# Value products taken unit by unit, index scores in PSUM, and three smaller edits in a three-branch decoder layer

## Chip, cores and metric

One Trainium2 chip, one core. The metric is the device time of one execution in microseconds. A run of the kernel before takes 537.79 us (median of three: 534.98, 537.79, 538.72).

## What is computed

One decoder layer over 512 tokens of width 1024. One input projection feeds three mixers side by side, whose results are gated, projected, merged and normalised. Cut to what this change is about:

```python
u = x @ w_in + b_in                               # split by columns into the parts below
# A: pooling with trailing windows 2, 4, 8, 16 on four groups of 128 channels
pooled = mean_over_window(a_x) - a_x              # the first w-1 tokens divide by their position
y_a = (pooled @ pool_w + b) * scale * silu(a_z)
# B: an indexer picks 128 keys for each query
score = sum_h relu(iq_h @ ik.T) * iw_h            # 8 index heads
sel = top_k(causal(score))
y_b = softmax(bq @ bk[sel].T / 8) @ bv[sel] * silu(b_z)     # 8 heads of 64
# C: compressed blocks, selected blocks and a window, 2 groups of 4 heads
k_cmp, v_cmp = mlp(blocks of 32 tokens)           # 31 blocks per group
o = g0 * softmax(cq @ k_cmp.T) @ v_cmp + g1 * softmax(cq @ ks.T) @ vs + g2 * softmax(cq @ kw.T) @ vw
y_c = o * silu(c_z)
m = sum over branches of sigmoid(g_branch) * (y_branch @ w_proj_branch)
out = layernorm(ALPHA * x + m @ w_o)
```

## The kernel before

**Dense work.** The projection's weights come as 53 tiles of 128 x 1024 (`load_w`): a DMA into `w_st`, a high part `w_h` by ACT (L93), a low part `w_l` by GpSimd (L95; by DVE for the first twelve). Every fp32 product is three matmuls (`mm3`, L68 to L70): high by high, high by low, low by high. Such a group of three, 512 columns wide, is the smallest piece of dense work; the projections are `d`, those of the merge `pp`, those of the output `wo`.

**Attention units.** A unit is one group of four heads and one block `j` of 128 queries, for a branch of C (names `c`, two branches `br`) or for B (names `b`). `Unit.front` makes the scores in PSUM (L442, `qkc`/`qkb`), DVE masks them and takes the least (L444), ACT exponentiates with that as bias (L449), DVE computes `r`, one over the sum (L453 to L457), ACT and DVE split the probabilities into two f16 parts (L461, L463), and SP's queue transposes them with a DMA (L470) into `ptc` or `ptb`, of which there are two buffers. A unit with `j` of 2 or 3 is made in two subunits of two heads. `Unit.back` multiplies the transposed parts by the values (L480) into an accumulator `acc`. `finish` (L535, DVE) reads the accumulator and writes `yb` or `yc`. All accumulators are two halves, used in turn, of one PSUM tile `ACC` that fills one bank:

```python
    ACC = pv.tile([128, 2, 2, 128], F32, name="acc2")
    turn = [0]
```

`Compressed` rides on the first branch of C: its scores (L506, or L502 and L503 for the last block), one exp over 128 x 32 blocks of four heads (L512, L513), and products of its own (L530) into the same accumulator with `VC`, the compressed values with the heads on the diagonal (L397).

**Order.** PE's order is the order of the program (`manual_schedule`). The order on the other engines is worked out by a scheduler from it. Dense work and merging lie in a stream `F` as generators that yield after every group; between pieces of attention `F.step(n)` issues n of them. The work list runs c units of group 0 (`j` 3, 2, 1, 0, each with two branches), c of group 1, then b units of group 0 (`j` 0 to 3) and of group 1. `flush` issues the backs: always two units together, once the second of the two is `LAG` = 2 subunits old. For C the two are the branches of one accumulator; for B they are two accumulators, b0 with b1 and b2 with b3, and the finish of the first stands between their products:

```python
            for _, un, (kind, g, j, br) in pair:
                for _ in un.back(br == 0):
                    n += 1
                if kind == "b":
                    finish(un.acc, j, zb[g], YB[g])
```

**Other places.** `index_scores` (L283): per index head a product of 128 x n into one of four PSUM banks (L290), a relu by ACT into an SBUF tile `rel` (L292), and an accumulation by DVE (L294, L296). The DVE top-k rounds (L305, L306, L309) are spread between subunits. `compress_v` (L382) writes `VC` with six DVE multiplications by a mask. `pool_x` (L555) makes the pooled group; its first w − 1 columns are made apart and copied in by DVE (L574).

Of the kernel before, what the change touches and what calls it, by code (L numbers as in the profile page):

```python
# [7 lines left out]
F32 = mybir.dt.float32  # L8
# [3 lines left out]
AF = mybir.ActivationFunctionType  # L12
OP = mybir.AluOpType
# [12 lines left out]
I_IQ, I_KK, I_CQ, I_KC, I_VC, I_CZ, I_BQ, I_BZ, I_AX, I_AZ, I_G = (  # L26
    1, 3, 5, 9, 10, 11, 15, 19, 23, 27, 31)
NTILES = I_G + 24
SMALL = (("posk", 32), ("posv", 32), ("pool_b", 4), ("pool_scale", 4), ("bmask", 4), ("rcnt", 16), ("rowv", 1),
         ("mcmp", 128), ("ident", 128))  # L30
EARLY = (0, I_KK)

# [2 lines left out]
def trunk(ctx, tc, a, out, dbg=None):  # L35
    nc = tc.nc
# [11 lines left out]
    def big(tag, name, dt=F32, shape=(128, 2, 512)):  # L48
        return bp.tile(list(shape), dt, tag=tag, name=name, bufs=BUFS[tag])
# [7 lines left out]
    def qps(name):  # L57
        return pq.tile([128, 512], F32, tag="pq", name=name)
# [18 lines left out]
    small = {}  # L77
# [23 lines left out]
    ps = qps("idle")  # L101
# [25 lines left out]
    bias = const("bias")  # L127
# [157 lines left out]
    def index_scores(j):  # L285
        n = (j + 1) * 128
        acc = cp.tile([128, n], F32, name=f"acc{j}")
        for h in range(8):
            ps = qps(f"is{j}{h}")[:, :n]
            nc.tensor.matmul(ps, QI[h][:, (j - 1) * 128:j * 128], KI[:, :n], start=True, stop=True)  # L290
            rel = big("b", "rel", F32, (128, 512))[:, :n]
            nc.scalar.activation(rel, ps, AF.Relu)  # L292
            if h == 0:
                nc.vector.tensor_scalar(acc, rel, IW[:, j, 0:1], None, op0=OP.mult)  # L294
            else:
                nc.vector.scalar_tensor_tensor(acc, rel, IW[:, j, h:h + 1], acc, op0=OP.mult, op1=OP.add)  # L296
            yield
        dg = acc[:, j * 128:n]
        nc.vector.tensor_add(dg, dg, cmask[:, 384:512])
        dbg(f"score{j}", acc)  # L300
        negm[j] = acc
# [11 lines left out]
    KCH = cp.tile([128, 2, 32], F32R, name="kch")  # L313
    KCL = cp.tile([128, 2, 32], F32R, name="kcl")
    VC = [cp.tile([128, 2, 4, 64], BF, name=f"vc{p}") for p in range(3)]

    CP = {}

# [62 lines left out]

    def compress_v():  # L382
        HH, HL, w2h, w2l = CP["v"] + W2[1]
        bmask = small["bmask"]
        v32 = sp.tile([128, 2, 64], F32, name="vc32", bufs=1)
        ps = dps("vc")[:, :128].rearrange("p (g d) -> p g d", g=2)
        for g in range(2):
            mm3(ps[:, g], HH[:, g].rearrange("p r n -> p (r n)"), HL[:, g].rearrange("p r n -> p (r n)"),
                w2h, w2l, True, True)
        nc.vector.tensor_scalar(v32, ps, vscale, 0.5, op0=OP.mult, op1=OP.mult)  # L390
        for p in range(3):
            v1 = sp.tile([128, 2, 64], BF, name="vc1", bufs=2)
            nc.vector.tensor_copy(v1, v32)
            if p < 2:
                nc.vector.tensor_sub(v32, v32, v1)
            for g in range(2):
                nc.vector.tensor_mul(VC[p][:, g], v1[:, g, None, :].to_broadcast([128, 4, 64]),  # L397
                                     bmask[:, :, None].to_broadcast([128, 4, 64]))
        yield


# [83 lines left out]
    class Compressed:  # L485
# [5 lines left out]
        def begin(self, j, Q, K):  # L491
            self.j = j
            self.s = sp.tile([128, 4, 32], F32, name="cs", bufs=1)
            self.mx = sm("cmx", 4, 2)
            self.scale = 0.125 if j == NT - 1 else -1.0
            if j == NT - 1:
                ps = dps("sc")[:, :128].rearrange("p (h n) -> p h n", h=4)
                for h in range(4):
                    q = Q[h // 2][:, h % 2, j * 128:(j + 1) * 128]
                    for z in range(2):  # L500
                        nc.tensor.matmul(ps[:, h], q, K[:, z, :32], start=z == 0, stop=z == 1)
                nc.vector.tensor_add(self.s, ps, mcmp[:, j, None].to_broadcast([128, 4, 32]))  # L502
                nc.vector.tensor_reduce(self.mx[:, :4], self.s, AX.X, OP.max)  # L503

        def score(self, h, ps):
            nc.vector.tensor_tensor_reduce(self.s[:, h], ps, mcmp[:, self.j], -0.125, 3e38, OP.add, OP.min,  # L506
# [2 lines left out]
        def probs(self):  # L509
            g, j, s = self.g, self.j, self.s  # L510
            den, r = sm("cden", 4, 2), sm("cr", 4, 2)
            nc.vector.tensor_sub(s, s, self.mx[:, :4, None].to_broadcast([128, 4, 32]))  # L512
            nc.scalar.activation(s, s, AF.Exp, scale=self.scale)  # L513
            nc.vector.tensor_reduce(den, s, AX.X, OP.add)
            nc.vector.reciprocal(r, den)
            nc.vector.tensor_mul(r, r, GS[:, j, 12 * g:12 * g + 12:3])
            if j == 0:
                nc.vector.tensor_scalar(r, r, rowv, None, op0=OP.mult)
            nc.vector.tensor_mul(s, s, r[:, :, None].to_broadcast([128, 4, 32]))
            p = sp.tile([128, 2, 4, 32], F16, name="cp", bufs=1)  # L520
            nc.scalar.activation(p[:, 0], s, AF.Copy)
            nc.vector.tensor_sub(p[:, 1], s, p[:, 0])
            self.pt = sp.tile([128, 2, 128], F16, name="cpt", bufs=2)
            nc.sync.dma_start_transpose(self.pt, p.rearrange("p z h n -> p (z h n)"))
# [32 lines left out]
    def pool_x(g):  # L557
        w = 2 << g
        ps, b = yield from dense(I_AX + g)
        x0 = big("b", "x0", F32, (128, 512))  # L560
        with tc.high_priority():
            hi(x0, ps, b)
        cur = x0
        for i in range(g + 1):
            nxt = big("b", "xs", F32, (128, 512))
            sft = 1 << i
            nc.gpsimd.tensor_add(nxt[:, sft:], cur[:, sft:], cur[:, :S - sft])
            nc.gpsimd.tensor_copy(nxt[:, :sft], cur[:, :sft])
            cur = nxt
        e = sm("pe", 16, 1)  # L570
        nc.vector.tensor_mul(e[:, :w - 1], cur[:, :w - 1], PL["rcnt"][:, :w - 1])
        nc.vector.tensor_sub(e[:, :w - 1], e[:, :w - 1], x0[:, :w - 1])
        nc.vector.scalar_tensor_tensor(x0, cur, 1.0 / w, x0, op0=OP.mult, op1=OP.subtract)
        nc.vector.tensor_copy(x0[:, :w - 1], e[:, :w - 1])  # L574
        ph = PL["x", g] = big("t", "ph", F32R)
        split(ph[:, 0], ph[:, 1], x0)

# [160 lines left out]
    mcmp, rowv = small["mcmp"].rearrange("p (j n) -> p j n", j=NT), small["rowv"]  # L738
# [38 lines left out]
    backs = []  # L777
    accs, cmps = {}, {}
    nsub = 0

    def flush(limit):

        while backs and (limit == 1000 or len(backs) > 1 and backs[1][0] <= limit):
            pair, n = backs[:2], 0
            del backs[:2]
            if limit == 1000:
                F.step(12)
            for _, un, (kind, g, j, br) in pair:
                if kind == "c":
                    F.until(("vscales",), ("compress_v",), ("f_zc", g, 0), ("f_zc", g, 1))  # L790
                else:
                    F.until(("f_zb", g, 0), ("f_zb", g, 1))
            for _, un, (kind, g, j, br) in pair:
                for _ in un.back(br == 0):
                    n += 1
                if kind == "b":
                    finish(un.acc, j, zb[g], YB[g])
                elif br == 1:
                    cmps[g, j].back(un.acc)
                    finish(un.acc, j, zc[g], YC[g])  # L800
                    if j == 0:
                        flags.add(f"c{g}")
                        if g == 1:
                            split_y(2, YC)
            F.step(0.3 * n)

    for w in work:
        kind, g, j, br = w
        if kind == "c":
# [6 lines left out]
            if br == 0:  # L816
                cmps[g, j] = Compressed(g)
            un = Unit(f"c{g}{j}{br}", accs[w[:3]], j, qc[g], kk[g][br], cmask[:, (3 - j) * 128:],
                      1 + 2 * br + g, gv[:, 4 * g:4 * g + 4, 1 + br], None if br else cmps[g, j])
        else:  # L820
# [3 lines left out]
            if j:  # L824
                tk_until(j)
            un = Unit(f"b{g}{j}", psum_acc(), j, qb[g], KB[0], cmask[:, 384:] if j == 0 else negm[j],
                      0, None)
        for u in range(un.nsub):
# [4 lines left out]
            nsub += 1  # L833
            F.step(2)
            flush(nsub - LAG)
        backs.append((nsub, un, w))
    flush(1000)
    F.rest()
    POOL[0] = False
# [60 lines left out]
    for t in range(NT):  # L900
        last = t == NT - 1
        for c0, c1 in ((512, 768), (768, 1024)) if last else ((512, 1024),):
            ps = dps("wo")
# [5 lines left out]
        mv, ve, y, e = sm("mv", 2), sm("ve", 1), sm("rs", 1), sm("nw", 1)  # L909
# [8 lines left out]
        if not last:  # L918
            c = cs.pop()
# [11 lines left out]
def layout(v):  # L931
    import numpy as np
    v = {k: np.asarray(x) for k, x in v.items()}
    x, w, b = v["x"][0], v["w_in"][0], v["b_in"][0]
# [17 lines left out]
    c = np.ascontiguousarray  # L952
# [15 lines left out]
    for n in "kv":  # L968
        p = v["cmp_pos_" + n][0].T
# [4 lines left out]
    f4 = np.float32  # L974
    t = np.arange(128)
    r["cmask"] = np.concatenate([np.zeros((128, 384), f4), np.where(t[None] <= t[:, None], 0, NEG).astype(f4)], 1)
    r["ident"] = np.eye(128, dtype=f4)
    n = np.arange(32)
    tt = (np.arange(4)[None, :] * 128 + t[:, None])[:, :, None]
    r["mcmp"] = np.where((16 * n + 31 <= tt) & (n < 31), 0, NEG).astype(f4)  # L980
    r["rowv"] = (t >= 31).astype(f4)[:, None]
    r["bmask"] = (t[:, None] // 32 == np.arange(4)[None]).astype(f4)
    r["rcnt"] = c(np.broadcast_to((1.0 / np.arange(1, 17)).astype(f4), (128, 16)))
    r["small"] = np.concatenate([r.pop(k).reshape(128, n) for k, n in SMALL], 1)
    return {k: c(x) for k, x in r.items()}
# [16 lines left out]
```

## Time and profile before

| | us |
|---|---|
| median of three runs | 537.79 |
| profiled execution | 536.65 |
| its span | 534.9 |
| outside the span | 1.75 |
| mean granted TensorE clock, share of full speed | 0.982 |

The profile follows one execution. A row of busy time says how long an engine worked in the span; a row of a wait says which engine stood idle ahead of which instruction, and whose instruction ended that idle time. PE is TensorE's matmul, PEld its weight load beside it. In names, buffer numbers are left out.

### The profile page before, as it was taken

How to read it: one execution, taken by the hardware profiler on the slowest of the kernel's cores; microseconds unless marked ns; L12 is line 12 of the kernel's file. 1: busy time of each engine (PE TensorE's matmuls, PEld its weight loads, DVE VectorE, ACT ScalarE, POOL GpSimd, SP SyncE). 2: the span in 40 equal slices, each digit the busy share in tenths (PEclk: the TensorE clock that was granted, in tenths of full speed). 3: DMA queues.
4: the chain of work that ended last, by engine and by line, in shares of the span. 5: the costliest groups of instructions: out<-in, count | busy, mean ns of one | idle time of the engine just before them, and what ended most of it. 6: DMA issues, size and time to landing. Idle time of an engine off the chain costs nothing. (4 is left out here: it accounts for less than half of the span.)

```text
span 534.9 us, 7764 instructions
## 1 busy us (share of the span) xinstructions
PE 510.4 (95%) x2718; PEld 423.7 (79%) x2718; DVE 380.2 (71%) x928; ACT 278.4 (52%) x561; POOL 218.5 (41%) x190
## 2 busy tenths in 40 slices
PE   8999999999999998999998995999899999999993
PEld 5899878888888886788887884887787888887883
DVE  5774798898769898997898879565653345554276
ACT  6783465667655666565546564575553245342000
POOL 0425433436553756153534534227651212116043
PEclk9999989999999999999999998899999999999997
DMA  8622331363854434364545636256444435463012
GB/s 286 256 79 80 112 126 60 87 148 86 183 139 123 119 85 117 63 181 124 140 121 104 132 110 145 49 138 138 119 119 134 141 137 187 148 205 110 1 69 89
DMA packets 82135, 66.72 MB, mean 125 GB/s; under 512 B 67184, under 2 KB 68656, under 8 KB 82096
## 3 DMA queue, kind: packets, MB, share of 16 engines
q1 hardware_dynamic: 74912, 40.54, 28.5%
q0 software_dynamic: 7184, 25.69, 16.1%
q8 instruction: 21, 0.34, 0.3%
q14 instruction: 18, 0.15, 0.1%
HBM read 47.87 MB, written 2.10 MB: 93 GB/s over the span
## 5 line engine op out<-in xcount | busy, mean ns | idle before, releaser
L68 PE MATMUL d<-xh,w_h 128*128 128x512 f32 (+1 forms) x424 | 167.5, 395 | 2.6 <-ACT z L153 2.2
L69 PE MATMUL d<-xl,w_h 128*128 128x512 f32 (+1 forms) x424 | 165.8, 391 | 0.0
L70 PE MATMUL d<-xh,w_l 128*128 128x512 f32 (+1 forms) x424 | 165.5, 390 | 0.0
L95 POOL TENSOR_TENSOR w_l<-w_st,w_h 128x1024 fp32r<-128x1024 f32 x41 | 99.5, 2428 | 127.1 <-ACT w_h L93 120.4
L68 PEld LDWEIGHTS d<-xh,w_h 128*128 128x128 f32 x424 | 80.5, 190 | 18.3 <-ACT z L153 2.6
L70 PEld LDWEIGHTS d<-xh,w_l 128*128 128x128 f32 x424 | 80.3, 189 | 16.9
L69 PEld LDWEIGHTS d<-xl,w_h 128*128 128x128 f32 x424 | 80.4, 190 | 14.1
L93 ACT ACTIVATE w_h<-w_st 128x1024 fp32r<-128x1024 f32 x53 | 56.2, 1060 | 36.9 <-DMA w_st<-in_wt_dram 20.5
L449 ACT ACTIVATE qkc<-qkc,nb 128x512 f32<-128x512 f32 (+3 forms) x64 | 32.0, 501 | 49.8 <-DVE nb L444 32.0
L95 POOL TENSOR_TENSOR wp_l<-wp_st,wp_h 128x512 fp32r<-128x512 f32 x16 | 20.8, 1297 | 48.3 <-ACT wp_h L93 48.3
L641 POOL TENSOR_TENSOR m<-m,tg 128x512 f32<-128x512 f32 x12 | 17.5, 1457 | 54.2 <-DVE tg L615 54.0
L463 DVE SCALAR_TENSOR_TENSOR pc<-qkc,r,pc 128x512 f16<-128x512 f32 (+3 forms) x64 | 32.4, 544 | 8.2 <-ACT pc L461 7.9
L461 ACT ACTIVATE pc<-qkc,r 128x512 f16<-128x512 f32 (+3 forms) x64 | 29.5, 525 | 15.1 <-DVE r L457 7.2
L444 DVE CUSTOM_DVE_ANT_0 qkc<-qkc,cmask 128x512 f32<-128x512 f32 (+3 forms) x64 | 31.2, 493 | 2.9 <-PE qkc L442 2.5
L449 ACT ACTIVATE qkb<-qkb,nb 128x128 f32<-128x128 f32 (+3 forms) x32 | 16.0, 499 | 23.1 <-DVE nb L444 22.8
L92 POOL DMA_DIRECT2D w_st<-in_wt_dram x41 | 23.3, 569 | 9.9 <-POOL w_l L95 5.9
L70 PE MATMUL wo<-woh,ml 128*128 128x512 f32 (+1 forms) x72 | 26.4, 367 | 0.6 <-DVE ml L65 0.6
L69 PE MATMUL wo<-wol,mh 128*128 128x512 f32 (+1 forms) x72 | 26.3, 366 | 0.0
L68 PE MATMUL wo<-woh,mh 128*128 128x512 f32 (+1 forms) x72 | 26.3, 365 | 0.0
L306 DVE MATCH_REPLACE8 acc<-m,acc 128x256 f32<-128x256 f32 (+2 forms) x48 | 25.9, 541 | 0.0
L305 DVE MAX8 m<-acc 128x8 f32<-128x256 f32 (+2 forms) x48 | 25.2, 548 | 0.1
L68 PE MATMUL pp<-yh,wp_h 128*128 128x512 f32 x64 | 25.1, 392 | 0.0
(249 smaller groups left out, 1015.3 us busy)
## 6 DMA issues: line engine op xcount, KB each, us to landing
w_st<-in_wt_dram POOLq DMA_DIRECT2D x41, 512.0 KB, 3.7
w_st<-in_wt_dram SPq DMA_DIRECT2D x12, 512.0 KB, 4.4
wp_st<-in_wp_dram POOLq DMA_DIRECT2D x16, 256.0 KB, 3.0
wo_st<-in_wo_dram SPq DMA_DIRECT2D x8, 512.0 KB, 3.5
xst<-in_xT_dram SPq DMA_DIRECT2D x8, 256.0 KB, 4.8
wp_st<-in_wp_dram SPq DMA_DIRECT2D x8, 256.0 KB, 2.6
z<-in_x_dram SPq DMA_DIRECT2D x4, 512.0 KB, 5.1
wvst<-in_wve_dram SPq DMA_DIRECT2D x4, 320.0 KB, 7.1
```

Source lines behind the costliest of these rows:

```text
L68: nc.tensor.matmul(ps, wh, rh, start=start, stop=False)
L69: nc.tensor.matmul(ps, wh, rl, start=False, stop=False)
L70: nc.tensor.matmul(ps, wl, rh, start=False, stop=stop)
L92: (nc.gpsimd if POOL[0] else nc.sync).dma_start(st, src)
L93: nc.scalar.activation(h[:, :n], st, AF.Copy)
L95: eng.tensor_sub(l[:, :n], st, f(h[:, :n]))
L305: nc.vector.max(m8, negm[j])
L306: nc.vector.match_replace(negm[j], m8, negm[j], MARK)
L444: nc.vector.tensor_tensor_reduce(sc[i], sc[i], self.mask, -0.125, 3e38, OP.add, OP.min, nb[:, i:i + 1])
L449: nc.scalar.activation(sc[i], sc[i], AF.Exp, scale=-1.0, bias=nb[:, i:i + 1], accum_out=den[:, i:i + 1])
L461: nc.scalar.activation(p[:, 0, i], sc[i], AF.Copy, scale=r[:, i:i + 1])
L463: self.last = nc.vector.scalar_tensor_tensor(p[:, 1, i], sc[i], r[:, i:i + 1], p[:, 0, i], op0=OP.mult, op1=OP.subtract)
```

## The change

Five edits. (1) Backs carry a count: the two branches of C stay together, a b unit goes alone, each when it is `LAG` subunits old; before the last backs 8 instead of 12 groups of the stream are stepped, for each back. (2) The relu of an index score is written over it in PSUM. (3) `VC` is zeroed by three GpSimd memsets at the start and filled by twelve GpSimd copies of 32 partitions x 2 x 64; the mask is gone. (4) The pooling edge is written in place, the rest from column w − 1. (5) The least compressed score is a bias of the exp, by head: four exps of 32 columns for one of 128, without the subtraction; for the last block the maximum is multiplied by −0.125 first.

```diff
-SMALL = (("posk", 32), ("posv", 32), ("pool_b", 4), ("pool_scale", 4), ("bmask", 4), ("rcnt", 16), ("rowv", 1),
+SMALL = (("posk", 32), ("posv", 32), ("pool_b", 4), ("pool_scale", 4), ("rcnt", 16), ("rowv", 1),
          ("mcmp", 128), ("ident", 128))
...
@@ index_scores
             nc.tensor.matmul(ps, QI[h][:, (j - 1) * 128:j * 128], KI[:, :n], start=True, stop=True)
-            rel = big("b", "rel", F32, (128, 512))[:, :n]
+            rel = ps
             nc.scalar.activation(rel, ps, AF.Relu)
...
     VC = [cp.tile([128, 2, 4, 64], BF, name=f"vc{p}") for p in range(3)]
+    for p in range(3):
+        nc.gpsimd.memset(VC[p], 0.0)
...
@@ compress_v
-        bmask = small["bmask"]
...
             if p < 2:
                 nc.vector.tensor_sub(v32, v32, v1)
-            for g in range(2):
-                nc.vector.tensor_mul(VC[p][:, g], v1[:, g, None, :].to_broadcast([128, 4, 64]),
-                                     bmask[:, :, None].to_broadcast([128, 4, 64]))
+            for h in range(4):
+                r = slice(32 * h, 32 * h + 32)
+                nc.gpsimd.tensor_copy(VC[p][r, :, h], v1[r])
...
@@ Compressed.begin (j == NT - 1)
                 nc.vector.tensor_reduce(self.mx[:, :4], self.s, AX.X, OP.max)
+                nc.vector.tensor_scalar(self.mx[:, :4], self.mx[:, :4], -0.125, None, op0=OP.mult)
...
@@ Compressed.probs
-            nc.vector.tensor_sub(s, s, self.mx[:, :4, None].to_broadcast([128, 4, 32]))
-            nc.scalar.activation(s, s, AF.Exp, scale=self.scale)
+            for h in range(4):
+                nc.scalar.activation(s[:, h], s[:, h], AF.Exp, scale=self.scale, bias=self.mx[:, h:h + 1])
...
@@ pool_x
-        nc.vector.tensor_sub(e[:, :w - 1], e[:, :w - 1], x0[:, :w - 1])
-        nc.vector.scalar_tensor_tensor(x0, cur, 1.0 / w, x0, op0=OP.mult, op1=OP.subtract)
-        nc.vector.tensor_copy(x0[:, :w - 1], e[:, :w - 1])
+        nc.vector.tensor_sub(x0[:, :w - 1], e[:, :w - 1], x0[:, :w - 1])
+        nc.vector.scalar_tensor_tensor(x0[:, w - 1:], cur[:, w - 1:], 1.0 / w, x0[:, w - 1:], op0=OP.mult,
+                                       op1=OP.subtract)
...
@@ flush
-        while backs and (limit == 1000 or len(backs) > 1 and backs[1][0] <= limit):
-            pair, n = backs[:2], 0
-            del backs[:2]
+        while backs and (limit == 1000 or len(backs) >= backs[0][3] and backs[backs[0][3] - 1][0] <= limit):
+            pair, n = backs[:backs[0][3]], 0
+            del backs[:len(pair)]
             if limit == 1000:
-                F.step(12)
+                F.step(8)
...
@@ the loop over the work list
-        backs.append((nsub, un, w))
+        backs.append((nsub, un, w, 2 if kind == "c" else 1))
```

PE around the backs of b0 and b1 of group 0, before. `ptb_3437` holds b0's transposed probabilities, `ptb_3509` b1's; `acc_152` is the one accumulator tile.

```order
L480 LDWEIGHTS vl
L480 MATMUL acc_152<-ptb_3437,vl 64x256
L480 LDWEIGHTS vh
L480 MATMUL acc_152<-ptb_3437,vh 64x256
L480 LDWEIGHTS vh
L480 MATMUL acc_152<-ptb_3437,vh 64x256
L480 LDWEIGHTS vh
L480 MATMUL acc_152<-ptb_3509,vh 64x256
L480 LDWEIGHTS vh
L480 MATMUL acc_152<-ptb_3509,vh 64x256
```

The products of b1 follow those of b0 directly. The same place after the change (lines are one further on, b0 is `ptb_3436`):

```order
L481 MATMUL acc_155<-ptb_3436,vh 64x256
L481 LDWEIGHTS vh
L481 MATMUL acc_155<-ptb_3436,vh 64x256
L443 MATMUL qkb_3634<-kb,bq_2532 128x384 x2
L68 MATMUL d_3599<-xh_85,w_h 128x512
L69 MATMUL d_3599<-xl_89,w_h 128x512
L70 MATMUL d_3599<-xh_85,w_l 128x512
L68 MATMUL d_3599<-xh_86,w_h 128x512
L69 MATMUL d_3599<-xl_90,w_h 128x512
```

Behind b0's products now stand scores of b2 and dense groups; b1's products come after four scores' matmuls and nine groups in all. Before the pair stood behind six groups and the last scores.

DVE around the finish of b0, before (`yb_3378` is written by both finishes, `acc_855` are the index scores in top-k):

```order
L453 RECIPROCAL r<-den 128x2
L306 MATCH_REPLACE acc_855<-m_3617,acc_855 128x512
L455 TENSOR_SCALAR r<-r 128x2
L463 SCALAR_TENSOR_TENSOR pb_3670<-qkb_3628,r,pb_3670 128x384
L463 SCALAR_TENSOR_TENSOR pb_3670<-qkb_3642,r,pb_3670 128x384
L305 MAX m_3676<-acc_855 128x8
L535 SCALAR_TENSOR_TENSOR yb_3378<-acc_152,yscale,zb_2642 128x2x128
L306 MATCH_REPLACE acc_855<-m_3676,acc_855 128x512
L309 TENSOR_SCALAR acc_855<-acc_855 128x512
L535 SCALAR_TENSOR_TENSOR yb_3378<-acc_152,yscale,zb_2642 128x2x128
```

And after (`acc_842` the index scores, `acc_155` the accumulator):

```order
L305 MAX m_3513<-acc_842 128x8
L306 MATCH_REPLACE acc_842<-m_3513,acc_842 128x512
L454 RECIPROCAL r<-den 128x2
L456 TENSOR_SCALAR r<-r 128x2
L537 SCALAR_TENSOR_TENSOR yb_3377<-acc_155,yscale,zb_2635 128x2x128
L445 ISA qkb_3634,nb<-qkb_3634,acc_685 128x384
L445 ISA nb 128x1
L464 SCALAR_TENSOR_TENSOR pb_3606<-qkb_3567,r,pb_3606 128x384
```

The finish of b0 has moved ahead of the masking of the next scores and of the split that is next in line, and stands directly behind an `r`.

GpSimd in the stretch of `compress_v`, after; before, this place holds only `w_l` and the DMA issues in turn.

```order
L95 TENSOR_TENSOR w_l<-w_st,w_h 128x1024
L92 DMA w_st<-in_wt_dram 128x1024
L399 COPY vc_149<-vc_1090 32x2x64 x4
L95 TENSOR_TENSOR w_l<-w_st,w_h 128x1024
L399 COPY vc_150<-vc_1097 32x2x64 x4
L92 DMA w_st<-in_wt_dram 128x1024
L399 COPY vc_151<-vc_1104 32x2x64 x4
L95 TENSOR_TENSOR w_l<-w_st,w_h 128x1024
```

Four copies stand ahead of a `w_l` three times, one time ahead of a weight's DMA too.

## Rows read from the trace of the kernel before

**Rows 1.** Busy time of each engine (us), share of the span, instructions, from the page.

```profile
PE 510.4 (95%) x2718; PEld 423.7 (79%) x2718; DVE 380.2 (71%) x928; ACT 278.4 (52%) x561; POOL 218.5 (41%) x190
```

**Rows 2.** PE's waits: us in total, times, longest.

```profile
PE acc L480 <- DVE yb L535: 8.0, 4, 5.5
PE d L68 <- ACT z L153: 2.2, 1, 2.2
...
PE cpk L69 <- DVE bkl L65: 1.2, 1, 1.2
```

**Rows 3.** Timeline, 328 to 334: start, us, engine, line, operation [idle before].

```profile
328.71 2.33 POOL L95 TENSOR_TENSOR w_l<-w_st,w_h 128x1024 fp32r<-128x1024 f32 x1 [3.87 <-ACT w_h L93]
329.01 2.06 DVE L455 TENSOR_SCALAR r<-r 128x2 f32<-128x2 f32 x1
...
333.43 0.47 DVE L535 SCALAR_TENSOR_TENSOR yb<-acc,yscale,zb 128x256 f32<-128x256 f32 x1
...
333.95 0.42 PE L480 MATMUL acc<-ptb,vh 128*64 128x256 f16 x2 [5.45 <-DVE yb L535]
```

**Rows 4.** Timeline of PE and DVE, parts of 335 to 407.

```profile
335.37 1.22 PE L442 MATMUL qkb<-kb,bq 128*128 128x512 f32 x2
...
365.25 0.30 PE L480 MATMUL acc<-ptb,vh 128*64 128x256 f16 x2 [0.58 <-DVE yb L535]
...
383.38 0.47 DVE L535 SCALAR_TENSOR_TENSOR yb<-acc,yscale,zb 128x256 f32<-128x256 f32 x1
383.91 0.30 PE L480 MATMUL acc<-ptb,vh 128*64 128x256 f16 x2 [1.42 <-DVE yb L535]
...
384.69 0.73 PE L442 MATMUL qkb<-kb,bq 128*128 128x512 f32 x2
...
385.26 0.39 PE L68 MATMUL d<-xh,w_h 128*128 128x512 f32 x1
...
385.72 0.39 PE L70 MATMUL d<-xh,w_l 128*128 128x512 f32 x1
...
406.44 0.30 PE L480 MATMUL acc<-ptb,vh 128*64 128x256 f16 x2
```

**Rows 5.** Stretches: us, then busy time of each engine (instructions), PE's granted clock.

```profile
core 0: us, PE busy (x) PEld busy (x) DVE busy (x) ACT busy (x) POOL busy (x), PEclk, DMA share, GB/s
210.90:214.90 4.00, 3.96 (x10) 3.16 (x11) 4.00 (x11) 1.66 (x3) 1.89 (x3) 0.57 0.85 180
...
333.90:337.60 3.70, 3.65 (x17) 2.86 (x17) 2.32 (x5) 0.18 (x1) 0.00 (x0) 0.50 0.47 106
```

**Rows 6.** Groups by line and form: busy us, mean ns of one, idle before.

```profile
L512 DVE TENSOR_TENSOR cs<-cs,cmx 128x128 f32<-128x128 f32 x8 | 6.8, 851 | 0.2
...
L449 ACT ACTIVATE qkb<-qkb,nb 128x128 f32<-128x128 f32 x8 | 2.7, 339 | 3.4 <-DVE nb L444 3.3
...
L449 ACT ACTIVATE qkb<-qkb,nb 128x512 f32<-128x512 f32 x8 | 5.3, 659 | 10.9 <-DVE nb L444 10.9
...
L380 POOL CAST ks<-kcl 128x32 fp32r<-128x32 f32 x2 | 1.0, 512 | 0.0
```

**Rows 7.** DMA issues: times, median us to landing.

```profile
ptb<-pb SPq DMA_TRANSPOSE x12, 3.7
```

**Rows 8.** Timeline of SP's queue, 399 to 400.5.

```profile
400.06 1.56 SPq L470 DMA_TRANSPOSE ptb<-pb  x1
```

**Rows 9.** Timeline of the index scores, 59 to 69.

```profile
59.33 2.39 POOL L95 TENSOR_TENSOR w_l<-w_st,w_h 128x1024 fp32r<-128x1024 f32 x1 [4.24 <-ACT w_h L93]
...
59.54 2.46 DVE L296 SCALAR_TENSOR_TENSOR acc<-rel,iw,acc 128x256 f32<-128x256 f32 x1
...
62.09 0.28 PE L290 MATMUL is<-ki,qi 128*128 128x256 f32 x1
...
67.97 0.49 DVE L296 SCALAR_TENSOR_TENSOR acc<-rel,iw,acc 128x256 f32<-128x256 f32 x1
...
68.28 0.34 PE L290 MATMUL is<-ki,qi 128*128 128x384 f32 x1
```

More of the change, by code (lines that the diff above doesn't have):

```diff
@@ L781, in flush @@
     def flush(limit):
-        while backs and (limit == 1000 or len(backs) > 1 and backs[1][0] <= limit):
-            pair, n = backs[:2], 0
-            del backs[:2]
+        while backs and (limit == 1000 or len(backs) >= backs[0][3] and backs[backs[0][3] - 1][0] <= limit):
+            pair, n = backs[:backs[0][3]], 0
+            del backs[:len(pair)]
             if limit == 1000:
-                F.step(12)
-            for _, un, (kind, g, j, br) in pair:
+                F.step(8)
+            for _, un, (kind, g, j, br), _ in pair:
                 if kind == "c":
@@ L792, in flush @@
                     F.until(("f_zb", g, 0), ("f_zb", g, 1))
-            for _, un, (kind, g, j, br) in pair:
+            for _, un, (kind, g, j, br), _ in pair:
                 for _ in un.back(br == 0):
@@ L981, in layout @@
     r["rowv"] = (t >= 31).astype(f4)[:, None]
-    r["bmask"] = (t[:, None] // 32 == np.arange(4)[None]).astype(f4)
     r["rcnt"] = c(np.broadcast_to((1.0 / np.arange(1, 17)).astype(f4), (128, 16)))
```

## Prediction

> **What bounds the kernel now.** I read the busy shares first: TensorE (PE) works 510.4 of 534.9 us, VectorE (DVE) 71%, ScalarE (ACT) 52%, GpSimd (POOL) 41% [rows 1]. Nothing but PE can set the time, and it has little idle to give back. So the second view is PE's own waits. The change touches one entry of it by its place in the program and another by the engine behind it: the value products wait 8.0 us in four pieces for the DVE instruction that finishes an accumulator; `cpk`, the compressed keys, waits 1.2 us for a DVE split. The 2.2 us for ACT's `z` is the only other one above 2 [rows 2]. No line of that view names GpSimd's `w_l`, a transpose or a shared scratch tile: what the change does to those starts from zero wait.
>
> Third, the timeline around the longest piece. PE's value products of unit b1 (group 0) start at 333.95 after 5.45 us of idle, 0.05 us behind the end of `yb` (333.43 + 0.47) [rows 3]. b0's products had ended by 333.95 − 5.45 = 328.50; its `yb` stood behind other work in DVE's order: an `r` that took 2.06 us for two numbers per row while GpSimd's `w_l` ran from 328.71 to 331.04, then two splits of b1's probabilities (L463) and a top-k step. The third pair has the same form: `yb` ends at 383.85 (0.47 long), PE starts at 383.91 after 1.42 us [rows 4]. The second pair waits 0.58 (at 365.25), which leaves 8.0 − 5.45 − 1.42 − 0.58 = 0.55 for the fourth: `yb`'s 0.47 and the signals, the least such a wait can be when a finish stands directly between two backs.
>
> Fourth, the clock behind the long piece. After 5.45 us of nothing the granted clock is 0.50 (1.2 GHz of 2.4) from 333.9 to 337.6, with 17 PE instructions in it [rows 5]. The twelve products take 333.95 to 335.37 = 1.42 us there and 383.91 to 384.69 = 0.78 us at full clock [rows 3, 4], a loss of 45%; half the clock would lose 50%. Of 3.65 busy us that is 1.65 to 1.85; I take 1.65, since the rate of real rows is nearer than the ratio of clocks. The matmuls behind 1.42 us of idle are not slowed (0.39 us each at 385.26 and 385.72) [rows 4], so only the first wait has this term.
>
> **The change, part by part.** (1) *Backs of b one at a time.* The products of a b unit go out as soon as it alone is due, so between two of them stand now four to nine groups of three dense matmuls and mostly scores too. In the order after the change the least that I find is between b2 and b3 of group 1: 1 + 4 + 4 groups. A group takes 0.69 us (385.26 to 385.72 is two matmuls of three) [rows 4], so 9 × 0.69 = 6.2 us; DVE needs 0.47 for `yb`, and stands behind one `r` at most in its new order. All four waits go: −8.0, and −1.65 of clock: −9.65 us. What is late next: nothing that the waits view lists; PE has dense work on both sides of each back. The smaller step before the last backs (8 for 12) only moves such groups from one side of a back to the other. If the cover goes, a wait is 0.55 per finish, eight finishes.
>
> DVE can be up to 2.06 us late by such an `r` [rows 3], and 6.2 us holds that three times. The Trainium skill ("SBUF — State Buffer", Who interferes with whom) says that a DVE operation in a two-port mode and a GpSimd one exclude each other for a whole instruction; the 2.06 us `r` beside a 2.33 us `w_l` agrees. By that rule the new place of `yb`, straight behind an `r`, is exposed to one such block each time, and the sum stays, since one block is shorter than the cover.
>
> The transposes that feed a back become the nearer risk. The last half of b3 in group 1 is issued at 400.06 [rows 8], a landing takes 3.7 at the median [rows 7]: 403.8. Its back comes after 14 groups and b2's 18 products instead of 17 groups: 406.44 − 3 × 0.69 + 18 × 0.065 (0.78 us for twelve) = 405.5 [rows 4]. Margin 1.7 us: kept. Transposes of the first units wait less for the tile than before (two buffers, free earlier).
>
> (2) *Index scores relu in place in PSUM.* The same 24 relus and 24 accumulations; a bank is now held until DVE has read it, not until ACT has. The bank of the product at 62.09 would be free at 68.46 (67.97 + 0.49), and the fourth product after it starts at 68.28: 0.2 us late [rows 9]. Bounds: −1.2 (below) and +2.2, the size of the `z` wait. I take 0, the nearer to +0.2.
>
> (3) *Compressed blocks by GpSimd.* Six DVE multiplications go, which only relieves DVE and is not counted; three memsets at the head of GpSimd's queue and twelve copies of 32 × 128 are added. No row shows such a copy: the cast of 128 × 32 takes 0.51, `w_l` of 128 × 1024 2.33 [rows 3, 6], so 12 × 0.51 = 6.1 us up to 12 × 2.33 = 28. I take 6.1: 128 elements per partition are nearer to 32 than to 1024. Four copies stand ahead of each of three `w_l` in the new order, and DVE's cast of `vc` ahead of them; PE's dense matmuls would wait behind `w_l`. GpSimd has 59% free, no wait for `w_l` exists, so 0; at 2.33 each, four copies delay a `w_l` by 9.3, and I allow a stall the size of `z`'s for that.
>
> (4) *Pooling edge in place.* Four tiny DVE copies go, none awaited by PE: 0.
>
> (5) *Least compressed score as bias.* DVE loses 8 subtractions, 6.8 us, and gains two small multiplications; ACT's one exp becomes four of 32 columns. From 0.339 at 128 and 0.659 at 512 the slope is 0.833 ns a column [rows 6], so 0.26 each, 1.04 for four against about 0.34 for one: +0.7 us × 8 = 5.6 us on an engine that is half idle. The new exps wait for the same minima as the subtraction did; behind them on ACT stand the `w_h` casts and `z`. Along the chain −0.85 and +0.7 cancel: 0. If ACT's cover is gone, each is 0.7.
>
> Sum: 536.65 (the profiled execution; 534.9 in the span, 1.75 around it) − 9.65 = 527.0. That execution lies 1.14 under the median of 537.79, from which the same sum gives 528.1. I say 527.5.
>
> **The rivals.**
> *A: DVE's relief gives more.* The row: DVE's accumulation at 59.54 takes 2.46 us while GpSimd's `w_l` runs (59.33 to 61.72), a like one at 67.97 takes 0.49 [rows 9]. Read as a mechanism: with `rel` in PSUM the accumulation reads one tile of SBUF, nothing holds it up, DVE is up to 2 us earlier, and the `cpk` wait of 1.2 [rows 2] on a DVE split goes, with as much clock behind it as behind `z` (0.57 over 4 us, 4.0 × 0.43 = 1.7) [rows 5]: 527.5 − 2.9 = 524.6. The same page of the Trainium skill says so: one input in SBUF does not contend, two do. Against it: one row of this size among many short ones, and several things feed that split. If `z`'s wait went too, 524.6 − 3.9 = 520.7.
>
> *B: transposes late.* For: single backs stand one margin from their transposes (1.7 us). If landings take twice the median, 7.4, b3's is 2.0 us late; two such units at 2.0 = 4.0: 531.5. Against: second units of pairs had this lag before, and no wait for a transpose is listed.
>
> *C: the c stage is upset.* ACT's +5.6 us and GpSimd's copies put two new stalls like `z`'s, 2.2 and 1.7 of clock each [rows 2, 5], into a stage in which PE hardly waits: 527.5 + 7.8 = 535.3. For: `z` shows that ACT can be the late one. Against: it is 48% free.
>
> *D, slower: PSUM banks of the index scores.* PE waits at every score whose bank DVE still reads. It already is 0.2 late by the rows above; from four stalls of 2.2 + 1.7 on it decides: 527.5 + 15.6 = 543.1, at six 550.9. For: DVE runs the accumulations in bursts. Against: one bank in the rows is past due, by 0.2 us only.
>
> That part (1) does not do what it says I exclude: in both pairs of rows PE starts 0.05 to 0.06 us after `yb` ends, so `yb` is what it waits for, and other work now stands there.
>
> **How the numbers follow.** Forecast (525 to 530) 0.60, A 0.12, B 0.12, C 0.11, D 0.05. One per cent, about what a measurement of this kernel can tell, is 5.4 us: under 532.4 is faster, over 543.2 slower. Faster: 0.60 + 0.12 + most of B (0.08) = 0.80; slower: D's greater part, 0.04; the same: 0.16. The range runs from between A's two prices, 522, to just under C's, 534; D, most of C and A's far end are left out, under 0.2.
>
> **What would show it.** Right: the waits view lists no value products behind `yb`, or under 1 us in all; PE is never at 0.50 clock between 320 and 330; `z` and `cpk` keep their places. A: `cpk` gone from the list. B: value products wait for a transpose. C: new waits for ACT or for `w_l` before 300. D: `is` products wait for DVE between 52 and 92. I am wrong if the four waits are gone and the time has not dropped by some 8 us, or if `yb` still heads the list.

## The result, and the profile after

| | before | after |
|---|---|---|
| median of four runs, us | 537.38 | 529.36 (529.06 to 529.60) |
| span of the profiled execution | 534.9 | 527.8 |
| mean granted TensorE clock | 0.982 | 0.991 |

The ratio is 0.9853, 95% interval 0.9817 to 0.9889: faster by 8 us, 6 to 10. The four waits of value products for `yb` are gone, and a new group of waits stands at the head of PE's list.

Busy time by engine, from the page after (before: [rows 1]).

```profile
PE 508.5 (96%) x2718; PEld 420.1 (80%) x2718; DVE 378.7 (72%) x912; ACT 281.5 (53%) x585; POOL 219.8 (42%) x205
```

PE's waits after (before: [rows 2]): us in total, times, longest.

```profile
PE qkc L443 <- DVE pc L464: 3.5, 3, 1.8
PE d L68 <- ACT z L153: 2.4, 1, 2.4
PE pp L68 <- DVE m L617: 1.2, 1, 1.2
...
PE cpk L69 <- DVE bkl L65: 0.5, 1, 0.5
```

The 8.0 us of L480 (now L481) are not in the list. `z` waits 2.4 (before 2.2), `cpk` falls from 1.2 to 0.5. New are 3.5 us in which scores (`qkc`) wait for L464, the split of the probabilities of an earlier subunit: it frees the PSUM bank that the scores go to.

Stretches after where before had the long wait and the half clock ([rows 3, 5]):

```profile
core 0: us, PE busy (x) PEld busy (x) DVE busy (x) ACT busy (x) POOL busy (x), PEclk, DMA share, GB/s
...
320.00:330.00 10.00, 10.00 (x50) 7.97 (x49) 9.38 (x24) 7.20 (x16) 5.23 (x4) 1.00 0.52 113
330.00:340.00 10.00, 10.00 (x54) 7.93 (x53) 9.02 (x20) 5.43 (x10) 5.89 (x4) 1.00 0.55 150
```

PE works all 10 us of both at full clock. The backs of b0 there, and the finish:

```profile
323.04 0.39 PE L70 MATMUL d<-xh,w_l 128*128 128x512 f32 x1
...
323.35 0.11 PEld L481 LDWEIGHTS <-vh 128*64 128x64 f16 x2 [0.35 <-issue]
...
323.60 0.28 PE L481 MATMUL acc<-ptb,vh 128*64 128x256 f16 x2
...
323.80 0.30 PEld L443 LDWEIGHTS qkb<-kb,bq 128*128 128x128 f32 x2 [0.20 <-issue]
...
327.45 0.46 DVE L456 TENSOR_SCALAR r<-r 128x2 f32<-128x2 f32 x1
...
327.81 0.47 DVE L537 SCALAR_TENSOR_TENSOR yb<-acc,yscale,zb 128x256 f32<-128x256 f32 x1
```

b0's products stand alone from 323.35 on, scores follow at 323.80. `yb` comes 4.0 us later, behind an `r` that was held up 0.3 us this time, and PE does not notice.

To see where the time went, I took the start of the same PE instruction in both traces (the twelfth index score, dense matmul number 313, 409, 889 and 1129, output matmul 193), which before start at 68.3, 108.6, 136.8, 311.3, 415.9 and 523.0, and subtracted. The change in each stretch, in us (minus is gained):

```
kernel                               to 68   to 109  to 137  to 311  to 416  to 523   sum
after (edits 1 to 5)                   0.0    -1.3    +4.3    -0.7    -9.1    -0.2    -7.1
e1  edit 1 alone                      +1.1    -1.3     0.0    +0.8    -9.1    +0.6    -7.9
e2  without edit 3                    -0.3    -1.4    +4.6    -1.5    -9.1    +0.8    -6.9
e3  without edit 5                    +0.4    -1.7     0.0    -1.0    -9.1    +0.7   -10.8
e4  without edit 2                    -1.2    +1.8     0.0    -1.4    -9.1    +1.0    -9.0
e5  after, splits first               -0.5    -1.6    +0.6    -0.9    -9.1    +1.0   -10.5
e6  after, low parts in halves        +1.8    -1.2    +1.1    -4.3    -9.1     0.0   -11.7
e7  without edit 1                    +0.4    -1.3    +4.1    -0.7    +1.9    -0.3    +3.9
e8  e5 and e6 together                +1.5    -1.2    +0.7    -4.8    -9.1    +0.2   -12.7
e9  before, low parts in halves       -1.4    -0.2     0.0    -2.7    -3.2    -0.2    -7.6
e10 e3, low parts in halves           +0.2    -1.4     0.0    -3.5    -9.1     0.0   -13.7
```

Each row is one profiled execution; what differs up to 68 us says nothing of the edits. Two columns matter most, to 137 and to 416: the b stretch repeats to 0.1 us, and a loss of 4.3 us in the c stage, which the prediction did not have, eats half of it. The experiments ask who makes that loss.

### The profile page after: what moved, and what is told of

Its sections match the earlier page's. It is cut to its first block, busy times and chain, and to the rows that moved or that the text cites. A ratio compares the mean times of both kernels' runs of the same rounds, so it can differ in the third digit from the quotient of the medians.

```text
span 527.8 us, 7784 instructions
## 1 busy us (share of the span) xinstructions
PE 508.5 (96%) x2718; PEld 420.1 (80%) x2718; DVE 378.7 (72%) x912; ACT 281.5 (53%) x585; POOL 219.8 (42%) x205
## 5 line engine op out<-in xcount | busy, mean ns | idle before, releaser
L95 POOL TENSOR_TENSOR w_l<-w_st,w_h 128x1024 fp32r<-128x1024 f32 x41 | 98.0, 2393 | 111.0 <-ACT w_h L93 109.9
L464 DVE SCALAR_TENSOR_TENSOR pc<-qkc,r,pc 128x512 f16<-128x512 f32 (+3 forms) x64 | 32.7, 545 | 10.8 <-ACT pc L462 10.6
L95 DVE TENSOR_TENSOR w_l<-w_st,w_h 128x1024 fp32r<-128x1024 f32 x12 | 15.8, 1323 | 13.4 <-ACT w_h L93 13.4
```

Of the source, the lines that this page charges most:

```text
L95: eng.tensor_sub(l[:, :n], st, f(h[:, :n]))
L464: self.last = nc.vector.scalar_tensor_tensor(p[:, 1, i], sc[i], r[:, i:i + 1], p[:, 0, i], op0=OP.mult, op1=OP.subtract)
```

## Experiments

**e1, edit 1 alone, and e7, all but edit 1.** Edit on the kernel before, and the reverse on the changed kernel:

```diff
-        backs.append((nsub, un, w))
+        backs.append((nsub, un, w, 2 if kind == "c" else 1))
```

(with the lines of `flush` that the diff above shows.) Expected of e1:

> The kernel before with edit 1 alone (b backs one at a time). Theory: the gain of the changed kernel in the b stretch (about 9.1 us) is this edit's alone, so the time is 9 us under before (528.5), the waits of value products for yb are gone, and the cpk wait stays at 1.2 us with no new score wait before 135 us. Rival: DVE's relief by the other edits carries part of the b stretch; then one or two waits for yb stay and the gain is 4 to 7 us.

Expected of e7:

> The changed kernel with edit 1 undone: pairs of b backs. Theory: edit 1 is worth 9.1 us whatever else is there and the other four cost about 2 us together, so 538.5, with the four waits for yb back (8 us) and half clock behind the longest. Rival: DVE's relief by edits 2 to 5 shortens the long wait too; then 533 to 536.

Measured: e1 529.75 us, ratio 0.9858 (0.9838 to 0.9878). e7 540.43, ratio 1.0071 (1.0047 to 1.0095): the other four edits alone make the kernel slower. PE's waits of e1, without one for `yb`:

```profile
PE d L68 <- ACT z L153: 2.2, 1, 2.2
PE pool L68 <- ACT ph L64: 1.4, 1, 1.4
...
PE cpk L69 <- DVE bkl L65: 1.0, 1, 1.0
```

and of e7:

```profile
PE acc L481 <- DVE yb L537: 9.7, 4, 7.1
PE qkc L443 <- DVE pc L464: 3.3, 3, 1.6
```

Edit 1 is the gain of the b stretch, −9.1 in each kernel that has it: e1's theory holds and both rivals fall. With 529.75 it is alone as fast as the changed kernel (529.36). e7's theory, that the edit is worth 9.1 whatever else is there, missed: 540.43 instead of 538.5. Beside the other edits it saves more, 11.0 in that stretch (+1.9 to −9.1), because there the longest wait is 7.1 instead of 5.5; the relief of DVE did not shorten it. Why DVE's chain stands 1.7 us later against PE in e7 was not followed up.

**e2, e3, e4: one of the other edits undone.** In the changed kernel, edit 3 back (six DVE multiplications for twelve GpSimd copies), edit 5 back (one exp behind a subtraction), edit 2 back (`rel` in SBUF). The edits are those hunks of the diff above with plus and minus exchanged; as one for all, e4:

```diff
-            rel = ps
+            rel = big("b", "rel", F32, (128, 512))[:, :n]
```

> The changed kernel with edit 3 undone (compressed blocks by DVE as before). Theory: the new waits of scores for the split of probabilities between 107 and 130 us (3.5 us, 4.3 us of lost time) come from GpSimd's copies, which move its low parts w_l beside DVE's critical instructions; they vanish and the time falls to about 525.5. Rival: edit 5's order of DVE and ACT makes them; then they stay and the time is 529 to 530.

> The changed kernel with edit 5 undone (one exp after a subtraction as before). Theory (GpSimd's copies make the new waits): they stay, the time is 529 to 530. Rival (edit 5 makes them): they vanish, about 525.5.

> The changed kernel with edit 2 undone (relu of the index scores into SBUF as before). Theory: the 1.3 to 1.9 us that the changed kernel is ahead at 77 us come from the accumulation with one SBUF input, which is not held up by w_l; the cpk wait is 1.2 again and the 77 us lead is gone: 530.7. Rival: the lead is only another order of DVE in that stretch; it stays, 529.4.

Measured: e2 529.58 us, ratio 0.9855 (0.9837 to 0.9873). e3 526.41, 0.9791 (0.9758 to 0.9824). e4 527.66, 0.9815 (0.9796 to 0.9835). The waits for scores in e2:

```profile
PE qkc L442 <- DVE pc L463: 2.7, 1, 2.7
```

In e3 there is none for scores; from its list:

```profile
PE d L68 <- ACT z L153: 2.2, 1, 2.2
...
PE cpk L69 <- DVE bkl L65: 0.2, 1, 0.2
```

The theory on GpSimd's copies falls: without them the loss is 4.6. It goes with edit 5 undone, as the rival said, but it goes with edit 2 undone too, where all of edit 5 is in place (that is why e4 came out 3 us under the 530.7 of its theory). So neither edit costs it by itself; the two together do. What they share is the scheduler, which works out DVE's order anew for each. In the changed kernel's timeline the split of one subunit's probabilities lies in two pieces:

```profile
102.45 0.75 DVE L464 SCALAR_TENSOR_TENSOR pc<-qkc,r,pc 128x512 f16<-128x512 f32 x1 [0.89 <-ACT pc L462]
...
103.12 0.69 DVE L445 CUSTOM_DVE_ANT_0 qkc<-qkc,cmask 128x512 f32<-128x512 f32 x1
...
103.50 2.39 POOL L95 TENSOR_TENSOR w_l<-w_st,w_h 128x1024 fp32r<-128x1024 f32 x1 [0.60 <-POOL vc L399]
...
103.72 2.32 DVE L396 TENSOR_TENSOR vc<-vc,vc 128x128 f32<-128x128 f32 x1
...
105.97 0.74 DVE L464 SCALAR_TENSOR_TENSOR pc<-qkc,r,pc 128x512 f16<-128x512 f32 x1
...
109.15 0.28 DVE L396 TENSOR_TENSOR vc<-vc,vc 128x128 f32<-128x128 f32 x1
...
113.47 0.73 PE L443 MATMUL qkc<-kw,cq 128*128 128x512 f32 x2 [1.53 <-DVE pc L464]
```

Between its halves (102.45 and 105.97) stand a masking and a subtraction of `compress_v`, L396, which takes 2.32 us beside GpSimd's `w_l`; the next one, without a `w_l` beside it, takes 0.28. What follows on DVE is later for it, down to the split that frees the bank for the scores at 113.47. In DVE's order of e3 and e4 the two halves follow each other, and the subtractions of `compress_v` come behind them.

On edit 2, from e4's waits:

```profile
PE d L68 <- ACT z L153: 2.3, 1, 2.3
PE cpk L69 <- DVE bkl L65: 1.4, 1, 1.4
```

`cpk` waits 1.4 there, and PE's clock is 0.57 from 72 to 80 in that trace. With edit 2 the `cpk` wait is 0.2 to 0.7 in the eight kernels that have it and the clock between 72 and 80 is 1.00; without it the wait is 0.9 to 1.4 in four, the clock low in three of them and full in e1. So edit 2 shortens the wait by some 0.6 us on the mean. What it is worth in time is not shown: the stretch to 109 gives −1.3 in e1 too, which lacks the edit, and the start of a run (the column to 68) moves by as much.

**e5: the order alone.** The loop of `compress_v` that makes the three parts, DVE's operations and GpSimd's copies, is queued behind the last split before it:

```diff
@@ compress_v
         nc.vector.tensor_scalar(v32, ps, vscale, 0.5, op0=OP.mult, op1=OP.mult)
-        for p in range(3):
...
+        with tc.issue_after(LAST[0].ins):
+            for p in range(3):
...
@@ Unit.front, behind the splits of a subunit
+            LAST[0] = self.last
...
```

> The changed kernel, with the DVE operations of compress_v queued behind the last split of probabilities before them; all else, and PE's order, as it is. Theory: edits 2 and 5 together only change DVE's order, a subtraction of compress_v that is held up 2.3 us by GpSimd's w_l stands between the two halves of a split, and the bank of scores is freed late. Then the first new wait (1.5 us at 113) goes, later ones shrink, the lead at 127 us is near -1.3 again, and the time is 525 to 527. Rival: ACT's four exps themselves delay the chain of the next unit; then the waits stay and the time is 529 to 530.

Measured: 525.19 us, ratio 0.9776 (0.9747 to 0.9805). DVE's timeline of e5 at this place, and what is left of the wait:

```profile
101.67 0.75 DVE L466 SCALAR_TENSOR_TENSOR pc<-qkc,r,pc 128x512 f16<-128x512 f32 x1 [1.15 <-ACT pc L464]
...
103.19 0.75 DVE L466 SCALAR_TENSOR_TENSOR pc<-qkc,r,pc 128x512 f16<-128x512 f32 x1
...
104.19 0.96 DVE L396 CAST vc<-vc 128x128 bf16<-128x128 f32 x1
```

```profile
PE qkc L445 <- DVE pc L466: 0.3, 1, 0.3
```

The loss falls from 4.3 to 0.6 with the same instructions in another order, edit 5's exps among them; PE's order is the same, the scheduler moved some instructions of ACT and GpSimd with DVE's. That the exps themselves delay the next unit is refuted for all but the 0.6 that is left.

**e6: the hold, and the order as it is.** GpSimd makes each low part in two operations:

```diff
-            eng.tensor_sub(l[:, :n], st, f(h[:, :n]))
+            for o in ((0, n // 2) if POOL[0] and n == 1024 else (0,)):
+                c = slice(o, o + n // 2 if POOL[0] and n == 1024 else n)
+                eng.tensor_sub(l[:, c], st[:, c], f(h[:, c]))
```

> The changed kernel with each GpSimd low part w_l made by two operations of 512 columns (1.3 us each) instead of one of 2.4. DVE's order in the stretch is unchanged up to 115 us. Theory: a DVE operation on SBUF is held up by the GpSimd operation that runs beside it, so the holds of 2.1 to 2.3 us at 103, 117 and 125 fall to 1.3 or less, the new waits shrink by 1 us or more each, and the time is 526 to 528. Rival: the waits come from the order alone; they stay within 0.5 us and the time is 529 to 530.

Measured: 523.69 us, ratio 0.9740 (0.9708 to 0.9772), faster than expected. At the same place in the order, and in its waits:

```profile
105.39 2.59 POOL L97 TENSOR_TENSOR w_l<-w_st,w_h 128x512 fp32r<-128x512 f32 x2 [0.60 <-POOL vc L401]
...
105.61 1.22 DVE L398 TENSOR_TENSOR vc<-vc,vc 128x128 f32<-128x128 f32 x1
```

```profile
PE d L68 <- ACT z L155: 0.8, 1, 0.8
...
PE qkc L445 <- DVE pc L466: 0.5, 1, 0.5
```

The held subtraction takes 1.22 instead of 2.32, the loss falls from 4.3 to 1.1. More is gained behind that: from 137 to 311 us 4.3, where `z` now waits 0.8 instead of 2.4 and the 1.2 us wait of `pp` is off the list. Not all of it is shorter holds: at 125, where an `r` was held before the second wait, the next `w_l` now starts (126.80) when the `r` is over (124.98, 0.15 us). So order and hold are both needed for the loss: a DVE instruction that PE needs soon, queued behind one that GpSimd holds up.

**e8, both cures, and e10, the halves without edit 5.**

> The changed kernel with both cures: DVE operations of compress_v behind the last split, and GpSimd's low parts in halves. Theory: both take away the same waits between 107 and 130 us (3.7 us by the order, 3.2 us by the halves), the halves also what they gave behind 200 us, so the time is near the better one of the two, 522 to 524. Rival: the two are independent and add up, 519 to 520.

> The changed kernel with edit 5 undone and GpSimd's low parts in halves. Theory: edit 5 costs only through DVE's order and the long holds; with the halves that is nearly gone (0.5 us of score waits were left), so the time is within 1 us of the halves alone, 523 to 524.5. Rival: ACT's 24 added exps cost by themselves; then it is 2 us or more below, under 522.

Measured: e8 523.72 us, 0.9744 (0.9710 to 0.9778). e10 523.75, 0.9772 (0.9720 to 0.9823). Neither differs from e6 by the median, as both theories said: with short holds the order matters little, and edit 5's 24 more ACT instructions cost nothing that shows in the medians. (The profiled executions of e8 and e10 are 1 to 2 us better than e6's, 1.1 of it in e10 in the stretch to 137; their medians are not.)

**e9: the halves on the kernel before.**

> The kernel before with GpSimd's low parts in halves and no other edit. Theory: the 2.06 us r ahead of yb falls to about 1.1, so the longest wait of value products falls from 5.5 to 4.5, the half clock behind it stays, and other holds shrink too: 533 to 536. Rival: the long wait is set by the order alone; it stays at 5.3 or more and the time at 536 to 538.

Measured: 529.67 us, ratio 0.9859 (0.9818 to 0.9900), 3 us better than expected and as much as the whole change. Around the longest wait (before: [rows 3]), and the sum of these waits:

```profile
323.26 2.49 POOL L97 TENSOR_TENSOR w_l<-w_st,w_h 128x512 fp32r<-128x512 f32 x2 [3.87 <-ACT w_h L93]
...
323.56 1.00 DVE L457 TENSOR_SCALAR r<-r 128x2 f32<-128x2 f32 x1
...
326.92 0.47 DVE L537 SCALAR_TENSOR_TENSOR yb<-acc,yscale,zb 128x256 f32<-128x256 f32 x1
...
327.44 0.30 PE L482 MATMUL acc<-ptb,vh 128*64 128x256 f16 x2 [3.19 <-DVE yb L537]
```

```profile
PE acc L482 <- DVE yb L537: 4.9, 4, 3.2
```

The `r` takes 1.00 instead of 2.06, `w_l` now two operations in 2.49, and the wait falls by 2.26, more than the 1.06 that the `r` loses. The other 1.20 is that the `r` starts earlier against PE: 0.69 us ahead of the end of b0's products (327.44 − 3.19 = 324.25), before 0.51 behind it. Which earlier piece of DVE's queue gave that was not traced. The wait of the third pair falls from 1.42 to 0.58 as well. So 3.2 of the 9.1 us in this stretch, about a third of what edit 1 gives, can be had without parting the pairs, by cutting GpSimd's long operation.

## Why the prediction came out

The time was right: 529.4 against 527.5, inside 522 to 534. The term that made it, edit 1, was right by its mechanism. That the other four edits came out within 2 us of their 0 is luck: a loss of 4.3 and gains of 2.0, neither of them in the sum, stand against each other.

*Edit 1, −9.65: the mechanism right, two sizes off.* The waits went, no other took their place, transposes were not late (rival B did not occur). The stretch gave −9.1 in all nine kernels that have the edit. The distances between PE's starts in both traces from 311 to 416 say how it comes about. The four waits were worth 8.7, not 8.0: the waits view counts from the end of the product before (5.45), but from start to start the gap was 5.73, where 0.11 is usual between pairs of products. The slow clock gave 1.67 (products 0.64, scores 0.26, the four distances behind them 0.77), as chosen. Against that stand four more switches between dense work and value products, for which the sum had no term: 0.32 instead of 0.23 on the way in (323.04 to 323.35 above) and 0.20 instead of 0.11 on the way out (the last pair starts at 323.60, the scores at 323.80), together 4 × 0.18 = 0.7. Each switch costs 0.13 more close by: the second matmul behind the products starts about 0.11 later than usual (dense work at 346.36 and 346.69, 0.33 apart instead of 0.23), the second pair of products 0.02 later. That is 0.31 for each parting, 1.25 in all: −8.7 − 1.67 + 1.25 = −9.1.

*Edit 2, 0: the hold of rival A is gone, its time is not shown.* The accumulation at 59.54, which took 2.46 us beside `w_l` [rows 9], takes 0.48 beside the same `w_l`:

```profile
59.33 2.40 POOL L95 TENSOR_TENSOR w_l<-w_st,w_h 128x1024 fp32r<-128x1024 f32 x1 [3.82 <-ACT w_h L93]
...
59.54 0.48 DVE L296 SCALAR_TENSOR_TENSOR acc<-is,iw,acc 128x256 f32<-128x256 f32 x1
```

After the change none of the 21 accumulations takes over 0.76 us; before, the one in [rows 9] took 2.46. The Trainium skill ("SBUF — State Buffer", Who interferes with whom) states that outside the two-port modes a DVE instruction with one input in SBUF does not contend with GpSimd, and that one with two contends with a GpSimd instruction that reads SBUF. The trace agrees: 0.48 us with one input in SBUF, 2.46 with two. The `cpk` wait fell by 0.7 and the slow clock behind it went; but the slow clock is gone in e1 too, without this edit. The bank of scores, rival D, was held no longer than PE's distance; no wait of `is` products is listed.

*Edit 3, 0.* Right, and the price was smaller than the one I chose:

```profile
L515 ACT ACTIVATE cs<-cs,cmx 128x32 f32<-128x32 f32 x32 | 9.5, 315 | 1.9 <-DVE cmx L508 1.0 <-DVE cmx L505 0.9
...
L399 POOL COPY vc<-vc 32x128 bf16<-32x128 bf16 x12 | 3.4, 286 | 6.0 <-DVE vc L394 4.2 <-DVE r L458 1.4
...
L317 POOL MEMSET vc<- 128x512 bf16 x3 | 1.4, 522 | 0.3 <-POOLq L993 0.3
```

A copy takes 0.29, not 0.51; the three memsets 1.4 in all at the start. In the trace the copies stand four ahead of one `w_l` (103.50) and eight ahead of the next (112.19), not four ahead of each of three. With the copies undone nothing changes (529.58, e2).

*Edit 4, 0.* No run has this edit alone or undone alone, so its worth is not shown; e1, without it and edits 2, 3 and 5, is as fast as the changed kernel.

*Edit 5, 0, with ACT's cover.* The step that failed is "Along the chain −0.85 and +0.7 cancel: 0". The chain itself cost little (0.6 us are left in e5, and e10 has the median of e6), but the edit, together with edit 2, gave DVE another order, and in that order an instruction that PE needs soon stood behind one that GpSimd holds up. An exp takes 0.31, not 0.26, so ACT's bill was 9.5 − 2.5 (eight exps of 0.31 before) = 7.0 us instead of 5.6. The Trainium skill ("ScalarE: Activation LUTs", What ACT_TABLE_LOAD costs) gives 280 ns and 0.833 ns a column for an activation with a pointer as bias, by estimate 307 ns for 32 columns: the trace agrees with 310 ns at the median. It does not for the rows of L449, in PSUM, through which the prediction drew its line: 339 ns at 128 columns, where the same figures give 387 by estimate.

*Rival C, 535.3, was right in the place and wrong in the cause.* It put the loss in the c stage, to ACT's and GpSimd's added work; GpSimd's made none of it (e2), ACT's at most the 0.6 that is left in e5. The two waits of size stood at 113 and 129; the second:

```profile
110.29 0.15 DVE L458 TENSOR_TENSOR r<-r,gs 128x2 f32<-128x2 f32 x1
...
124.96 2.39 POOL L95 TENSOR_TENSOR w_l<-w_st,w_h 128x1024 fp32r<-128x1024 f32 x1 [0.62 <-ACT w_h L93]
...
125.20 2.16 DVE L458 TENSOR_TENSOR r<-r,gs 128x2 f32<-128x2 f32 x1
...
127.45 1.27 ACT L462 ACTIVATE pc<-qkc,r 128x512 f16<-128x512 f32 x2 [1.92 <-issue]
...
128.51 0.75 DVE L464 SCALAR_TENSOR_TENSOR pc<-qkc,r,pc 128x512 f16<-128x512 f32 x1
...
129.31 0.65 PE L443 MATMUL qkc<-ks,cq 128*128 128x416 f32 x2 [1.79 <-DVE pc L464]
```

`r` is 0.15 us of work (at 110.29, with no `w_l` beside it), here 2.16 us beside `w_l`; ACT's scaling, DVE's split and PE's next scores follow one after the other. I had used such a hold as the cause of the 5.45 us wait and did not ask where else the new order of DVE would put one. The forecast stood because 4.3 was lost here, 2.0 was gained in the stretches before and behind, and edit 1 is the greater part: −1.3 + 4.3 − 0.7 − 9.1 − 0.2 = −7.1 in the span (before rounding), 8.0 by the medians.

## What to carry to other kernels

Where a scheduler sets the order of the engines beside a bound one, an edit that touches none of its instructions can still cost it: compare the new order of those engines, and look there for an instruction that the bound engine needs soon standing behind one that is often held up. Where two engines hold each other up, cut the long operation of the one that nobody waits for: the halves took 0.2 us more of GpSimd's idle time for each tile, and gave 7.4 us to the kernel before (537.1 to 529.7) and 5.7 to the changed one (529.4 to 523.7, which no version here beats clearly). A pair of products with a finish between them is better parted by work that is needed anyway, at 0.3 us for each parting here.

## What the runs showed of the hardware

A DVE operation of two numbers per row takes 0.15 to 0.17 us alone and up to 2.2 us beside a GpSimd operation of 2.4 us; with GpSimd's operation cut in two, the held ones shown here take 1.0 to 1.2. Held were operations with all inputs in SBUF (L396, L458, and with one input L455); one with PSUM for one of two inputs (L296 after the change) was not. Nor was every operation with one input in SBUF: none of the 38 reciprocals (L454 after) takes over 0.18 us, though 12 of them lie wholly inside a GpSimd tensor operation. Two halves of 512 columns take 2.5 to 2.7 us where the whole takes 2.4. Value products start two at a time, 64 columns each, pairs 0.11 us apart. PE's granted clock was 0.50 after 5.45 us of idle and 1.00 after 1.42 us [rows 4, 5]; but before the change it was 0.50 from 75 to 78 us too, where the wait ahead, for `cpk` at 72.07, was 1.16 us. The length of the wait alone does not tell which it will be.
